# Scan head of a hybrid attention and RWKV-7 trunk: loads reordered, one receptance projection moved ahead of the first slot

## The chip, the cores and the metric

The kernel runs on one NeuronCore of a Trainium2 chip. The metric is the device time of one execution in microseconds (us); lower is better. Five engines work side by side, each on its own list of instructions: PE (TensorE, matrix products; PEld are its weight loads), DVE (VectorE), ACT (ScalarE), POOL (GpSimd) and SP (SyncE), which in this kernel issues every DMA. They wait for one another by semaphores only.

## The reference

Two layers, each of feed-forward, mixer, feed-forward. The mixer of the second layer is RWKV-7 in both directions, and the change lies in it. Cut to what matters here (512 tokens, 1024 channels, 16 heads of 64):

```python
xr, xw, xk, xv, xa, xg = (x + xx * mix[i] for i in range(6))
r = xr @ w_rkv[0]                 # "receptance"
k = xk @ w_rkv[1]
v = xv @ w_rkv[2]
wl = w0 + einsum(tanh(einsum(xw, w1)), w2)
decay = exp(-exp(-softplus(-wl) - 0.5))
a = sigmoid(a0 + einsum(einsum(xa, a1), a2))
...
def step(state, inp):
    r_t, w_t, k_t, v_t, a_t, b_t = inp
    sa = einsum('zbhij,zbhj->zbhi', state, a_t)
    state = state * w_t[..., None, :] + sa[..., None] * b_t[..., None, :] + v_t[..., None] * k_t[..., None, :]
    return state, einsum('zbhij,zbhj->zbhi', state, r_t)
```

Then come a group norm, a bonus term, a gate and a projection by `w_out`.

## The kernel before, in words

The trunk is cut into stages in a row: input, first layer, first feed-forward of the second layer, `rwkv_project` (which ends at about 1432 us of the profile), `Scan` (1432 to about 1870 us), the output projection and the last feed-forward. `rwkv_project` makes k, the decays, the gate and other inputs of the scan and stores them in DRAM: `d_k`, `d_lw` (logarithms of the decays), `d_ah`, `d_iv`, `d_xr`, `d_xv`, `d_g`. Of the receptances it makes only those of head pair 0 (`d_r`); pairs 1 to 7 are made inside the scan.

`Scan` handles the 16 heads as 8 pairs (`hp` 0 to 7), with 8 chunks of 64 tokens in each of two directions (`z`). The work of a pair is split into threads, Python generators whose `yield` ends a step:

- `load(hp)`: k, iv and the raw a2 by DMA, then a2's split into a high and a low part (`a2u`).
- `front(hp, z)` (letters f0, f1): the decay tile `lw` by DMA, a product with `tri` into a PSUM bank of tag a, exponentials on ACT (`e`, `e2`), a three-matmul product of `a2u` with `ah`, then DVE work that builds `ar` and `bk`. It has six steps for z = 0.
- `grams(hp, z)` (g0, g1): products of `bk` and `ar` into banks g, masked by DVE into a unit `xs`, small copies by ACT (`qd`, `qc`), DMAs of halves of the unit (`az<-xs`, then `xs<-ar`).
- `tails` (t0, t1), `values` (v: first a DMA of the weights `wv`, then v from `xv` and `wv`, one of 8 channel chunks a step), `bonus` (b), `invert` (i: one DVE transpose, then 62 small POOL instructions), `inverted` (k), `merge` (j), `turn` (n), `chain` (c), `outputs` (d) and others.
- `receptances` (r): all projections of r for pairs 1, 4, 6, 7, 2, 3, 5. Its DMAs come first (8 chunks of `xr` into `az2` and units 8 and 9, the weights of pair 1 into unit 4, 8 chunks of `xv`, weights of pairs 4, 6 and 7 into units 5 to 7, weights of pairs 2, 3 and 5 into `vt` tiles). Then each projection takes four steps of two channel chunks, in bank y or m, and ends with a copy by ACT (`yt` or `yh`) and a DMA to `d_r`.

A slot n mixes threads of several pairs; the string `SEQ[n]` is the order, one letter a step. Slots -2 and -1 are the lead-in, 0 to 7 the rest. In the scan the orders of PE, ACT and DVE are exactly that of the program (`MANUAL_SCAN`); SP's and POOL's are set by a scheduler at build time, and on the chip each engine runs its list in that order. A DMA that waits on SP therefore holds all DMAs behind it. All DMAs go into one queue; SP uses eight semaphores in turn, so that a DMA waits until the one eight places before it has landed.

Ahead of slot -2, `run` does the whole of `load(0)`, the split of `ah` and the whole of `front(0, 0)`. `unit()` loads the start value `zs` of an inversion.

Of the kernel before, what the change touches and what calls it, by code (L numbers as in the profile page):

```python
# [18 lines left out]
P = 128  # L19
D = 1024  # L20
S = 512
FF = 2816
NF = FF // P
ND = D // P
NT = S // P
# [26 lines left out]
WR_FIRST = (1, 4, 6, 7)  # L52
# [7 lines left out]
SEQ = {  # L60
# [22 lines left out]
def chunks(ap):  # L83
    return ap.rearrange("p (c t) -> p c t", t=CH)
# [900 lines left out]
class Scan:  # L985
# [53 lines left out]
    def receptances(self):  # L1039

        nc = self.nc
        one = lambda ap: ap.rearrange("p a b c d -> p (a b c d)")
        az = self.az[2].rearrange("p a b c -> p (a b c)")
        xr = [h[:, i * S : (i + 1) * S] for h, n in ((az, 4), (one(self.units[-2][0]), 2), (one(self.units[-1][0]), 2)) for i in range(n)]
        for c in range(ND):
            nc.sync.dma_start(xr[c], self.dram["xr"][:, c, :])
        w = {}

        def load(hp, ap):
            w[hp] = ap.rearrange("p (c f) -> p c f", c=ND)  # L1050
            nc.sync.dma_start(w[hp], self.w_r[:, hp * P : (hp + 1) * P].rearrange("(c p) f -> p c f", p=P))

        for hp, i in zip(WR_FIRST, (4, 5, 6, 7)):
            load(hp, one(self.units[i][0]))
            if hp == 1:
                for c in range(ND):
                    nc.sync.dma_start(self.xv[:, c, :], self.dram["xv"][:, c, :])
        rest = [hp for hp in range(1, ND) if hp not in WR_FIRST]
        order = WR_FIRST + tuple(rest)
        while rest:  # L1060
            pair, rest = rest[:2], rest[2:]
            vt = self.tile("vt", [P, NC, 2, 2, CH], 2)
            for i, hp in enumerate(pair):
                load(hp, one(vt)[:, i * D : (i + 1) * D])
        for i, hp in enumerate(order):
            pr = self.k.bank("ym"[i % 2])
            for c in range(ND):
                self.wide(pr, w[hp][:, c, :], xr[c], c == 0, c == ND - 1)
                if c % 2 and c < ND - 1:
                    yield  # L1070
            t = self.tile(("yh", "yt")[hp % 2], [P, S])
            nc.scalar.activation(t, pr, AF.Copy)
            nc.sync.dma_start(self.dram["rkv"][0][:, hp, :], t)
            if hp == order[-1]:
                self.clear(2)
            yield
# [9 lines left out]

    def run(self, late, lead, ln):
        with self.k.tc.manual_schedule(engines=MANUAL_SCAN):
            raw = self.tile("e", [P, S], 2)
            for dst, src in ((raw, self.dram["ah"]), (self.tri, self.consts["tri"])):  # L1090
                self.nc.sync.dma_start(dst, src)
            list(self.load(0))
            self.k.split(self.ah[:, 0, :], self.ah[:, 1, :], raw)
            list(self.front(0, 0))
            for n in ("mask", "onesb"):
                self.nc.sync.dma_start(getattr(self, n), self.consts[n])
            self.zs = []
            for _ in range(2):
                self.unit()
            self.rs, self.out = self.receptances(), self.outs()  # L1100
            self.led, self.stored = [], 0
            for n in range(-2, HEADS // 2):
                if n == HEADS // 2 - 1:
                    self.early.tile([P, 56], F32, name="pad")
                    self.opened.close()
                    late.enter_context(self.k.early())
                    self.lw = self.leads(lead, ln)
                self.slot(n)
            self.ending = self.finish(HEADS // 2 - 1)
            next(self.ending)  # L1110
# [77 lines left out]
    def load(self, hp):  # L1188
# [16 lines left out]
        p.units, p.ar, p.bk = [], [], []  # L1205
        yield

    def front(self, hp, z):

        k, nc, tile_ = self.k, self.nc, self.tile  # L1210
        p = self.st[hp]
        way = slice(None, None, -1) if z else slice(None)
        if z == 0:
            p.r = tile_("r", [P, S], 2)
            nc.sync.dma_start(p.r, self.dram["rkv"][0][:, hp, :])
        lw = tile_("lw", [P, NT, P], 2)
        nc.sync.dma_start(lw, self.dram["lw"][:, z, :, hp * P : (hp + 1) * P])
        pi = k.bank("a")
        for t in range(NT):
            nc.tensor.matmul(pi[:, t * P : (t + 1) * P], lw[:, t, :], self.tri[:, z, :], start=True, stop=True)  # L1220
        yield
        e = tile_("e", [P, S], 2)
        nc.scalar.activation(e, pi, AF.Exp)
        e2 = tile_("e2", [P, S], 2)
        nc.scalar.activation(e2, pi, AF.Exp, scale=-1.0)
        yield
        pa = k.bank("a")
        k.mm3(pa, p.a2u[:, 0, z, :], p.a2u[:, 1, z, :], self.ah[:, 0, :], self.ah[:, 1, :], True, True)
        th = tile_("th", [P, S], 2)
        nc.scalar.activation(th, pa, AF.Tanh, scale=0.5, bias=k.col(C_A0H + z, hp))  # L1230
        ar = tile_("ar", [P, NC, 2, CH], 2)
        bk = tile_("bk", [P, NC, 2, CH], 2)
        at, rt = ar[:, way, 0, :], ar[:, way, 1, :]
        bt, kt = bk[:, way, z, way], bk[:, way, 1 - z, way]
        kc, ec = chunks(p.k), chunks(e)
        if z == 0:
            a1, a0, k1, k0, e1 = at[:, :, 1:], at[:, :, 0:1], kc[:, :, 1:], kc[:, :, 0:1], ec[:, :, : CH - 1]
        else:
            a1, a0, k1, k0, e1 = at[:, :, : 0 : -1], at[:, :, 0:1], kc[:, :, : CH - 1], kc[:, :, CH - 1 :], ec[:, :, 1:]
        nc.vector.scalar_tensor_tensor(a1, k1, k.col(C_NKK, hp), e1, ALU.mult, ALU.mult)  # L1240
        nc.vector.tensor_scalar(a0, k0, k.col(C_NKK, hp), None, ALU.mult)
        end = 0 if z else CH - 1
        ends = ec[:, way, end : end + 1]
        for h in range(2):
            nc.scalar.activation(p.pc[HALF[z], :, h : h + 1], ends[HALF[h]], AF.Copy)
        yield
        nc.vector.tensor_tensor(rt, chunks(p.r), ec, ALU.mult)
        if z == 0:
            nc.vector.scalar_tensor_tensor(p.iv, p.k, k.col(C_KKH, hp), p.iv, ALU.mult, ALU.mult)
        kz = tile_("kz", [P, S], 2)  # L1250
        nc.scalar.activation(kz, th, AF.Identity, scale=k.col(C_KA1, hp), bias=k.col(C_KA2, hp))
        yield
        nc.vector.tensor_tensor(kz, kz, p.k, ALU.mult)
        nc.vector.tensor_tensor(kt, chunks(kz), chunks(e2), ALU.mult)
        yield
        nc.vector.tensor_tensor(e2, p.iv, e2, ALU.mult)
        nc.vector.scalar_tensor_tensor(bt, chunks(th), 1.0, chunks(e2), ALU.add, ALU.mult)
        p.ar.append(ar)
        p.bk.append(bk)
        if z:  # L1260
            yield
            nc.vector.tensor_tensor(kz, p.kz, kz, ALU.add)
        p.kz = kz
        yield
# [436 lines left out]
```

## Time and profile before

| | |
|---|---|
| Time, median of 3 runs | 2250.02 us (2245.41 to 2254.24) |
| Profiled execution | 2249.58 us, of it the span of the instructions 2247.8 us |
| PE busy over the span | 2169.0 us (96%) |
| DVE, ACT, POOL busy | 48%, 43%, 63% |
| DMA | 328.82 MB, 146 GB/s on average |
| Granted TensorE clock, mean | 0.983 of full speed |

The time is a little longer than the span, since an execution also starts and ends outside the instructions. Times inside the profile count from the span's start. A row of the timeline gives start, duration, engine, line of the kernel, operation, tile written <- tiles read, count, and in brackets the idle time of the engine just before and what ended it.

### The profile page before, as it was taken

The page shows a single profiled execution, that of the slowest core. Times are in us where ns is not written, and L with a number is a line of the kernel's source. Part 1 is how long each engine was busy: PE and PEld are TensorE (multiplying, and loading weights), DVE is VectorE, ACT ScalarE, POOL GpSimd, SP SyncE. Part 2 cuts the span into 40 slices and gives each one's busy share as a digit, 9 for nine tenths or more (in the row PEclk, how much of TensorE's full clock was granted, in tenths as well). Part 3 has the DMA queues.
Part 4 walks back from the last instruction along what each step waited for, and adds up shares of the span by engine and source line. Part 5 has one row for each costly group of instructions (what it writes and reads, how often), then busy time and mean ns, then how long its engine had stood idle before and what let it go on. Part 6 is the DMA issues. An engine that isn't in the chain of part 4 may idle for free.

```text
span 2247.8 us, 35130 instructions
## 1 busy us (share of the span) xinstructions
PE 2169.0 (96%) x13784; PEld 1707.8 (76%) x13784; DVE 1068.3 (48%) x1549; ACT 973.8 (43%) x1706; POOL 1425.7 (63%) x1237
## 2 busy tenths in 40 slices
PE   8999999999999999999999988699999998999998
PEld 7888888887888888888888875435667656888886
DVE  2333356276423333743333698425778645232345
ACT  3333345376333333443333435336777633333333
POOL 6878855554487886588887433144776722888854
PEclk9999999999999999999999999799999999999999
DMA  6444463432344445354444534764454642544443
GB/s 199 143 145 145 143 229 97 135 89 91 103 141 150 145 141 174 132 181 137 141 141 132 196 123 155 268 162 117 126 137 111 206 149 94 159 141 141 141 169 122
DMA packets 350497, 328.82 MB, mean 146 GB/s; under 512 B 48458, under 2 KB 277450, under 8 KB 350332
## 3 DMA queue, kind: packets, MB, share of 16 engines
q1 hardware_dynamic: 350332, 326.58, 46.6%
q8 instruction: 108, 1.77, 0.3%
q14 instruction: 57, 0.47, 0.1%
HBM read 262.26 MB, written 47.74 MB: 138 GB/s over the span
## 4 chain that ended last, share of the span: by engine, by line
PE 83%; DVE 7%; DMA 4%; ACT 3%; issue 2%; POOL 1%; SPq 0%; DVEq 0%; ACTq 0%; POOLq 0%
PE bank L800 16%; PE bank L225 16%; PE bank L226 16%; PE bank L227 16%; PE bank L288 4%; PE a L990 3%; PE y L990 1%; PE g L1279 1%; DVE tmp L606 1%; PE m L990 1%; PE bank L1155 1%; DMA late<-in_ffn_w_out_dram 1%; PE g L990 1%; POOL w L221 1%; DMA wv<-in_w_rkv_dram 1%
## 5 line engine op out<-in xcount | busy, mean ns | idle before, releaser
L221 POOL TENSOR_TENSOR w<-raw,w 128x1024 fp32r<-128x1024 f32 (+2 forms) x203 | 507.2, 2500 | 248.3 <-ACT w L220 235.2
L226 PE MATMUL bank<-xT,w 128*128 128x512 f32 x1416 | 551.5, 389 | 1.7 <-DVE xT L221 1.7
L225 PE MATMUL bank<-xT,w 128*128 128x512 f32 x1416 | 552.5, 390 | 0.0
L227 PE MATMUL bank<-xT,w 128*128 128x512 f32 x1416 | 551.2, 389 | 0.0
L220 ACT ACTIVATE w<-raw 128x1024 fp32r<-128x1024 f32 x207 | 218.4, 1058 | 325.5 <-POOL ts L771 126.2
L422 DVE SCALAR_TENSOR_TENSOR ar<-bank,tmp 128x512 f32<-128x512 f32 x88 | 60.9, 692 | 585.1 <-PE bank L227 576.2
L226 PEld LDWEIGHTS bank<-xT,w 128*128 128x128 f32 x1416 | 265.9, 188 | 56.6 <-DVE xT L221 2.5
L227 PEld LDWEIGHTS bank<-xT,w 128*128 128x128 f32 x1416 | 265.8, 188 | 55.1
L225 PEld LDWEIGHTS bank<-xT,w 128*128 128x128 f32 x1416 | 265.9, 188 | 54.3
L1368 POOL TENSOR_TENSOR tm<-qs,zs 128x126 f32<-128x126 f32 (+22 forms) x248 | 104.9, 423 | 133.1 <-DVE qs L1361 83.9
L800 PE MATMUL bank<-wx,an 128*128 128x512 f32 x792 | 187.3, 389 | 0.0
L800 PEld LDWEIGHTS bank<-wx,an 128*128 128x128 f32 x792 | 148.7, 188 | 30.8
L800 PE MATMUL bank<-w,ring 128*128 128x512 f32 x720 | 168.8, 390 | 2.1 <-POOL w L221 2.1
L221 POOL TENSOR_TENSOR wx<-ra,wx 128x512 fp32r<-128x512 f32 x132 | 166.8, 1291 | 3.0 <-ACT wx L220 3.0
L221 DVE TENSOR_TENSOR ring<-ar,ring 128x1024 fp32r<-128x1024 f32 x44 | 122.8, 2792 | 81.3 <-ACT ring L220 81.2
L800 PEld LDWEIGHTS bank<-w,ring 128*128 128x128 f32 x720 | 134.9, 188 | 31.5 <-POOL w L221 3.2
L420 ACT ACTIVATE tmp<-bank 128x512 f32<-128x512 f32 x88 | 52.6, 598 | 231.0 <-PE bank L227 231.0
L221 POOL TENSOR_TENSOR ring<-raw,ring 128x1024 fp32r<-128x1024 f32 x28 | 68.2, 2445 | 96.7 <-ACT ring L220 96.6
L1370 POOL TENSOR_TENSOR zs<-zs,tm 128x126 f32<-128x126 f32 (+22 forms) x248 | 112.6, 454 | 19.4
L220 ACT ACTIVATE wx<-ra 128x512 fp32r<-128x512 f32 x132 | 82.9, 633 | 72.0 <-PE bank L800 67.8
L225 PE MATMUL bank<-xT,ring 128*128 128x256 f32 (+1 forms) x352 | 104.2, 304 | 9.8 <-ACT xT L220 3.7
L221 POOL TENSOR_TENSOR w<-late,w 128x1024 fp32r<-128x1024 f32 x30 | 75.6, 2525 | 58.8 <-ACT w L220 58.8
(284 smaller groups left out, 3779.0 us busy)
## 6 DMA issues: line engine op xcount, KB each, us to landing
raw<-in_ffn_w_in_dram SPq DMA_DIRECT2D x176, 512.0 KB, 3.9
ra<-in_ffn_w_out_dram SPq DMA_DIRECT2D x44, 1024.0 KB, 5.0
late<-d_late SPq DMA_DIRECT2D x34, 512.0 KB, 5.3
late<-in_ffn_w_out_dram SPq DMA_DIRECT2D x28, 512.0 KB, 4.6
raw<-in_w_qkv_dram SPq DMA_DIRECT2D x24, 512.0 KB, 3.9
d_late<-ts SPq DMA_DIRECT2D x44, 256.0 KB, 3.3
d_late<-ra SPq DMA_DIRECT2D x44, 256.0 KB, 2.0
xs<-ar SPq DMA_DIRECT2D x64, 128.0 KB, 2.4
```

Of the source, the lines that this page charges most:

```text
L220: self.hi = self.nc.scalar.activation(h, raw, AF.Copy).ins
L221: self.lo = (eng or self.nc.vector).tensor_tensor(l, raw, h.bitcast(F32), ALU.subtract).ins
L225: nc.tensor.matmul(out, wh, xh, start=start, stop=False)
L226: nc.tensor.matmul(out, wh, xl, start=False, stop=False)
L227: nc.tensor.matmul(out, wl, xh, start=False, stop=stop)
L288: nc.tensor.matmul(acc[t, h], a, u[:, i, h * 512 : (h + 1) * 512], start=first and n == 0, stop=last and n == 2)
L420: nc.scalar.activation(s, pg, AF.Silu)
L422: nc.vector.scalar_tensor_tensor(raw[:, 3:7:3] if j else raw[:, 0:8:7], halves_of(pu), 0.5, halves_of(s), ALU.mult, ALU.mult)
L800: self.nc.tensor.matmul(acc, lhs, u[:, i], start=bool(first) and m == 0, stop=last and m == 2, skip_group_check=more)
L990: self.nc.tensor.matmul(out[hs], w[:, hs], x, start=start, stop=stop)
L1368: nc.gpsimd.tensor_tensor(tv, qs[:, s, 0:s].rearrange("p (a o) -> p a o", o=1).broadcast_to([P, s, n]), zs[:, s : s + 1, c0:].broadcast_to ...
L1370: nc.gpsimd.tensor_tensor(zs[:, 0:s, c0:], zs[:, 0:s, c0:], tv, ALU.add)
```

## The change

1. The head's DMAs are in another order in the program. The decay tile of `front(0, 0)` (`fetch(0, 0)`) and `tri` come first, then k, iv and a2 of pair 0, then `ah`, the receptance tile of pair 0 (`receptance(0)`), the first `xr` chunk, the weights of the first projection, the other `xr` chunks, and among them the decay tile of `front(0, 1)` (`fetch(0, 1)`), `mask` and `onesb`. `xv` and the other projection weights follow at the first `r` step of the head.
2. The four `r` steps of the first projection (pair 1) are done ahead of slot -2, between the steps of `front(0, 0)`: the order is f, then the split of `ah`, then `f f r r f r f r f`.
3. Four `r` steps are taken out of `SEQ[-1]` (9 before, 5 now). Their number over the head and the two slots stays at 28 that do something, so every later projection moves four steps forward.

```diff
-    -1: "f1 v g0 k f1 g0 g0 v r r f1 k r f1 f1 r j f1 g0 l l r g1 r n r g0 g1 f0 g1 j g1 f0 f1 r t0 g1 g1 n g0 v t0 v "
-       "v v f0 v b t1 i f0 t1 v n v f0 f0 r b",
+    -1: "f1 v g0 k f1 g0 g0 v r r f1 k r f1 f1 r j f1 g0 l l r g1 n g0 g1 f0 g1 j g1 f0 f1 t0 g1 g1 n g0 v t0 v "
+       "v v f0 v b t1 i f0 t1 v n v f0 f0 b",
...
@@ receptances
-        for c in range(ND):
-            nc.sync.dma_start(xr[c], self.dram["xr"][:, c, :])
...
+        def chunk(c):
+            nc.sync.dma_start(xr[c], self.dram["xr"][:, c, :])
+
+        chunk(0)
         for hp, i in zip(WR_FIRST, (4, 5, 6, 7)):
             load(hp, one(self.units[i][0]))
-            if hp == 1:
+            if hp == WR_FIRST[0]:
+                for c in range(1, ND):
+                    chunk(c)
+                    if c == 2:
+                        self.fetch(0, 1)
+                        for n in ("mask", "onesb"):
+                            nc.sync.dma_start(getattr(self, n), self.consts[n])
+                yield
                 for c in range(ND):
                     nc.sync.dma_start(self.xv[:, c, :], self.dram["xv"][:, c, :])
@@ run
-            raw = self.tile("e", [P, S], 2)
-            for dst, src in ((raw, self.dram["ah"]), (self.tri, self.consts["tri"])):
-                self.nc.sync.dma_start(dst, src)
-            list(self.load(0))
-            self.k.split(self.ah[:, 0, :], self.ah[:, 1, :], raw)
-            list(self.front(0, 0))
-            for n in ("mask", "onesb"):
-                self.nc.sync.dma_start(getattr(self, n), self.consts[n])
-            self.zs = []
+            self.rs, self.out, self.zs, self.lws, self.rts = self.receptances(), self.outs(), [], {}, {}
+            self.fetch(0, 0)
+            self.nc.sync.dma_start(self.tri, self.consts["tri"])
+            load, start = self.load(0), self.front(0, 0)
+            next(load)
+            raw = self.tile("e", [P, S], 2)
+            self.nc.sync.dma_start(raw, self.dram["ah"])
+            self.receptance(0)
+            next(self.rs)
+            next(load)
+            next(start)
+            self.k.split(self.ah[:, 0, :], self.ah[:, 1, :], raw)
+            for name in "f f r r f r f r f".split():
+                next(start if name == "f" else self.rs)
+            assert next(load, 1) == 1 and next(start, 1) == 1
             for _ in range(2):
                 self.unit()
-            self.rs, self.out = self.receptances(), self.outs()
...
+    def fetch(self, hp, z):
+        lw = self.lws[hp, z] = self.tile("lw", [P, NT, P], 2)
+        self.nc.sync.dma_start(lw, self.dram["lw"][:, z, :, hp * P : (hp + 1) * P])
+
+    def receptance(self, hp):
+        r = self.rts[hp] = self.tile("r", [P, S], 2)
+        self.nc.sync.dma_start(r, self.dram["rkv"][0][:, hp, :])
```

**SP at the head.** What SP issues from the raw `ah` (tile `e`) on, before. The tiles `xs_10779` and, later, `xs_10799`, `xs_10801`, `xs_10790` are units 4 to 7 as homes of projection weights; `az_10807`, `xs_10803` and `xs_10794` are the homes of the `xr` chunks:

```order
L1091 DMA e<-d_ah 128x512
L1354 DMA zs<-in_eye_dram 128x512 x2
L1311 DMA wv<-in_w_rkv_dram 128x8x128
L1217 DMA lw<-d_lw 128x4x128
L1193 DMA k<-d_k 128x512
L1195 DMA iv<-d_iv 64x512 x2
L1197 DMA a2r<-in_a_dram 128x2x128
L1046 DMA az_10807<-d_xr 128x512 x4
L1046 DMA xs_10803<-d_xr 128x512 x2
L1046 DMA xs_10794<-d_xr 128x512 x2
L1051 DMA xs_10779<-in_w_rkv_dram 128x8x128
L1057 DMA xv<-d_xv 128x512 x8
```

And now, from the last `xr` chunks to the k tile of pair 1 (the `xr` chunks, the weights of pair 1, `lw`, `mask` and `onesb` stand ahead of this piece, right behind `ah`):

```order
L1052 DMA xs_10794<-d_xr 128x512 x2
L1066 DMA xv<-d_xv 128x512 x8
L1049 DMA xs_10799<-in_w_rkv_dram 128x8x128
L1049 DMA xs_10801<-in_w_rkv_dram 128x8x128
L1049 DMA xs_10790<-in_w_rkv_dram 128x8x128
L1049 DMA vt<-in_w_rkv_dram 128x8x128 x3
L1378 DMA zs<-in_eye_dram 128x512 x2
L1335 DMA wv<-in_w_rkv_dram 128x8x128
L1207 DMA k<-d_k 128x512
```

`wv`, the weights of the first `values`, stood third behind `ah`; it now stands behind all `xr`, all `xv` and all seven projection weights.

**PE at the head.** Before, from the first product of `front(0, 0)` to the first product of `values(0)`:

```order
L1220 MATMUL a<-tri,lw 128x128 x4
L225 MATMUL a<-ah,a2u 128x512
L226 MATMUL a<-ah,a2u 128x512
L227 MATMUL a<-ah,a2u 128x512
L1279 MATMUL g<-ar,bk 128x128 x8
L1220 MATMUL a<-tri,lw 128x128 x4
L225 MATMUL a<-ah,a2u 128x512
L226 MATMUL a<-ah,a2u 128x512
L227 MATMUL a<-ah,a2u 128x512
L990 MATMUL y<-az_10807,xs_10779 64x512 x8
L1279 MATMUL g<-ar,bk 128x128 x8
L990 MATMUL a<-xv,wv 64x512 x2
```

Now, from the last product of `front(0, 0)` to the same product of `values(0)`:

```order
L227 MATMUL a<-ah,a2u 128x512
L990 MATMUL y<-az_10807,xs_10779 64x512 x8
L990 MATMUL y<-xs_10803,xs_10779 64x512 x4
L990 MATMUL y<-xs_10794,xs_10779 64x512 x4
L1303 MATMUL g<-ar,bk 128x128 x8
L1244 MATMUL a<-tri,lw 128x128 x4
L225 MATMUL a<-ah,a2u 128x512
L226 MATMUL a<-ah,a2u 128x512
L227 MATMUL a<-ah,a2u 128x512
L990 MATMUL m<-az_10807,xs_10799 64x512 x8
L1303 MATMUL g<-ar,bk 128x128 x8
L990 MATMUL a<-xv,wv 64x512 x2
```

The whole projection of pair 1 stands ahead of the first gram, and the second projection (weights `xs_10799`) is where the first one began.

**PE in slot -1.** Before, from the first matmuls of `merge(0)` to the tails of pair 1 (L990 rows with `vt` are receptance steps):

```order
L1401 MATMUL p<-qs,qc 32x32 x32
L1279 MATMUL g<-ar,bk 128x128 x8
L990 MATMUL m<-xs_10794,vt 64x512 x4
L1279 MATMUL g<-ar,bk 128x128 x8
L990 MATMUL y<-az_10807,vt 64x512 x8
L1220 MATMUL a<-tri,lw 128x128 x4
L1408 MATMUL p<-qd,qc 32x32 x32
L1279 MATMUL g<-ar,bk 128x128 x8
L990 MATMUL y<-xs_10803,vt 64x512 x4
L1302 MATMUL g<-ident,bk 128x128 x4
```

Now:

```order
L1425 MATMUL p<-qs,qc 32x32 x32
L1303 MATMUL g<-ar,bk 128x128 x8
L990 MATMUL y<-xs_10794,vt 64x512 x4
L1303 MATMUL g<-ar,bk 128x128 x8
L1244 MATMUL a<-tri,lw 128x128 x4
L1432 MATMUL p<-qd,qc 32x32 x32
L1303 MATMUL g<-ar,bk 128x128 x8
L1326 MATMUL g<-ident,bk 128x128 x4
```

Three receptance steps are gone from here; the fourth, `y<-xs_10794,vt`, stood at the slot's end, ahead of the bonus product. The orders of DVE and POOL are as before; ACT's has only its copies of the projections (`yt`, `yh`) at other places. SP in slot -1 no longer reads a receptance tile back (`r<-d_r`) between iv and the first `az<-xs`, since that tile's read now stands earlier.

More of the change, by code (lines that the diff above doesn't have):

```diff
@@ L1213, in front @@
         if z == 0:
[L1214 to L1217, printed above, removed]
+            if hp:
+                self.receptance(hp)
+            p.r = self.rts.pop(hp)
+        if (hp, z) not in self.lws:
+            self.fetch(hp, z)
+        lw = self.lws.pop((hp, z))
         pi = k.bank("a")
```

## The prediction

> **What bounds the kernel now.** I read the shares by engine first: PE is busy 96% of the span, so PE's own idle time and its slow clock are what an edit of the scan's head can win or lose. Then I cut the head out by stage. Columns: stretch and its length, busy time (count) of PE, PEld, DVE, ACT, POOL, granted clock, DMA share, GB/s.
>
> ```profile
> core 0: us, PE busy (x) PEld busy (x) DVE busy (x) ACT busy (x) POOL busy (x), PEclk, DMA share, GB/s
> 1432.00:1465.00 33.00, 16.04 (x72) 9.31 (x70) 11.57 (x19) 9.18 (x21) 0.00 (x0) 0.59 0.98 306
> 1465.00:1545.00 80.00, 80.00 (x569) 34.26 (x567) 25.37 (x40) 35.65 (x87) 25.62 (x64) 1.00 0.53 143
> 1440.00:1475.00 35.00, 25.79 (x137) 13.65 (x138) 15.76 (x26) 12.83 (x34) 0.00 (x0) 0.72 1.05 305
> ```
>
> In the 33 us of the head PE works 16 and at 0.59 of its clock, while the DMA engines are full. In the 80 us behind it PE is busy without a gap at full clock, so whatever delays the start of that stretch delays all of it. PE's waits in the head (us in total, times, longest), and its timeline:
>
> ```profile
> PE a L1220 <- DMA lw<-d_lw: 8.2, 1, 8.2
> PE g L1279 <- DVE bk L1257: 4.8, 1, 4.8
> PE y L990 <- DMA xs<-in_w_rkv_dram: 3.9, 1, 3.9
> ```
>
> ```profile
> 1440.42 2.05 PE L1220 MATMUL a<-tri,lw 128*128 128x128 f32 x8 [8.16 <-DMA lw<-d_lw]
> ...
> 1443.56 0.63 PE L227 MATMUL a<-ah,a2u 128*128 128x512 f32 x1
> 1449.03 2.08 PE L1279 MATMUL g<-ar,bk 64*128 64x128 f32 x16 [4.85 <-DVE bk L1257]
> ...
> 1453.45 0.40 PE L227 MATMUL a<-ah,a2u 128*128 128x512 f32 x1
> 1457.79 6.38 PE L990 MATMUL y<-az,xs 128*64 128x512 f32 x16 [3.94 <-DMA xs<-in_w_rkv_dram]
> 1464.10 1.16 PE L1279 MATMUL g<-ar,bk 64*128 64x128 f32 x16
> 1465.19 1.08 PE L990 MATMUL a<-xv,wv 128*64 128x512 f32 x4
> ```
>
> The three waits are 17 us. Two end with a DMA in a full queue. The first product of `values` (1465.19) does not wait today: its weights `wv` were issued early.
>
> **The change part by part.**
>
> *The decay tile first, the projection in the gap.* The lw wait of 8.2 us shrinks, but what follows needs `ah`, which is issued at about the same place, so `front(0, 0)` does not end earlier. The four receptance steps then fill the wait for DVE's bk and part of the wait for weights. They are no gain by themselves: they hold up the first gram until the last `xr` chunk is there. What counts is when PE comes to the next point that DMA decides.
>
> *The load of `wv`.* It is now behind all `xr`, `xv`, all seven projection weights and the two `zs`. The queue serves in order: a 64 KB transfer issued behind two big weights took 6.3 us.
>
> ```profile
> 1464.89 1.68 SPq L1051 DMA_DIRECT2D vt<-in_w_rkv_dram  x1
> 1466.67 1.63 SPq L1291 DMA_DIRECT2D az<-xs  x1
> ```
>
> ```profile
> vt<-in_w_rkv_dram SPq DMA_DIRECT2D x1, 512.0 KB, 7.6
> az<-xs SPq DMA_DIRECT2D x1, 64.0 KB, 6.3
> ...
> k<-d_k SPq DMA_DIRECT2D x3, 256.0 KB, 5.0
> iv<-d_iv SPq DMA_DIRECT2D x6, 128.0 KB, 5.0
> a2r<-in_a_dram SPq DMA_DIRECT2D x3, 128.0 KB, 4.1
> ```
>
> From the head's first load to `wv` the new queue holds what the old one held up to its second `vt` weight, less k, two iv and a2r of pair 1 (256 + 256 + 128 = 640 KB), plus the third `vt` weight (512 KB). That is 128 KB less, 0.4 us at 305 GB/s. The old second `vt` weight landed at 1464.89 + 7.6 = 1472.5, so `wv` lands at 1472.1. PE is there long before: between the second projection's weights and `wv` stand 2560 KB of weights, 512 KB of `zs` and `wv` itself, 3584 KB or 12.0 us at 305 GB/s, and PE has between them two receptance steps (3.65 us for such an x16 row at full clock, below) and a gram (1.16). It stands about 7 us at the first product with `wv`, and behind that product, in program order, stand all other grams of slot -2, the inversion on POOL and the rest. That product was at 1465.19: **+6.9 us**. The bounds: 300 to 320 GB/s and the missing k and iv move the landing by about 2.5 us either way, 4.4 to 9.4.
>
> How this stands to PE's work: at 1465.19 today PE has done two receptance steps, at the new point six. Slot -2 has 19 steps before and after, so its length is the same 80 us stretch of PE work, and the four steps come back only in slot -1.
>
> *The clock.* After a wait PE restarts slow. Today's example is in slot -1:
>
> ```profile
> 1553.04 0.79 PE L225 MATMUL a<-ah,a2u 128*128 128x512 f32 x1 [2.66 <-DVE bon L1330]
> ...
> 1673.01 1.08 PE L990 MATMUL a<-xv,wv 128*64 128x512 f32 x4 [2.35 <-DMA wv<-in_w_rkv_dram]
> ```
>
> ```profile
> 1553.00:1559.00 6.00, 5.96 (x33) 3.65 (x33) 2.56 (x7) 1.93 (x4) 5.06 (x13) 0.51 0.28 89
> 1670.00:1680.00 10.00, 7.65 (x115) 5.44 (x115) 6.66 (x14) 6.38 (x18) 8.71 (x17) 1.00 0.45 136
> ```
>
> A wait of 2.66 us is followed by 6 us at 0.51, which costs 6 x 0.49 = 2.9 us; one of 2.35 us is followed by none. A wait of 7 us is beyond both, and at 1465.19 today the clock is already full: **+2.9 us** (0 if it recovered at once, 2.9 by the row). [...]
>
> *Four steps less in slot -1.* At full clock they are 1.8 us each, 7.2 us in all, and PE is busy there:
>
> ```profile
> 1522.95 1.94 PE L990 MATMUL m<-xs,vt 128*64 128x512 f32 x8
> ...
> 1525.91 3.65 PE L990 MATMUL y<-az,vt 128*64 128x512 f32 x16
> ...
> 1532.81 1.94 PE L990 MATMUL y<-xs,vt 128*64 128x512 f32 x8
> ```
>
> But the slot's end is not PE's. The last wait is the 2.66 us above, for DVE's bon, and DVE had itself waited 10.7 us for a DMA:
>
> ```profile
> 1545.53 0.74 DVE L1240 SCALAR_TENSOR_TENSOR ar<-k,cols,e 128x504 f32<-128x504 f32 x1 [10.74 <-DMA xs<-ar]
> ```
>
> That DMA is the last of a chain on SP, `az<-xs`, its landing, `xs<-ar`, three times over:
>
> ```profile
> 1527.58 1.14 SPq L1195 DMA_DIRECT2D iv<-d_iv  x2
> 1529.53 0.33 SPq L1215 DMA_DIRECT2D r<-d_r  x1
> 1529.94 1.38 SPq L1291 DMA_DIRECT2D az<-xs  x2
> ...
> SPq L1073 <- ACT az L1412: 1.4, 1, 1.4
> ...
> SPq L1292 <- DMA az<-xs: 1.8, 1, 1.8
> ```
>
> Fewer PE steps do not shorten the landings. What shortens is the place of `r<-d_r`, which no longer stands between iv (done 1528.72) and `az<-xs` (1529.94), 1.2 us, and the 1.4 us for ACT's az copy, since the products ahead of it move up by two steps. **-2.6 us**; bounds 0 (the landings decide) and 7.2 (PE decides). The steps taken out covered that wait, so PE will stand idle there longer than 2.66 us; its restart is already slow today.
>
> *The rest.*
>
> ```profile
> 1471.85 0.60 ACT L1072 ACTIVATE yt<-y 128x512 f32<-128x512 f32 x1
> ```
>
> I cost it at nothing: the copies `yt` and `yh` on ACT (0.6 us each; ACT is busy 35.65 of 80 us), the earlier `mask` and `onesb` (needed only with the first gram), and the later k, iv, a2 of pair 1, which land 640 KB or 2.2 us behind `wv`, ahead of their first use some 20 us on.
>
> *Sum* on the profiled execution (2249.58 us, of it 2247.8 the span): 6.9 + 2.9 - 2.6 = +7.2, so 2256.8 us. The median of the runs shown is 0.4 us above that execution, so I round to **2257 us**, slower by 0.3%. About 0.5% (11.2 us) is what a measurement of this kernel can tell from no change, and this is within it.
>
> **The rivals.**
>
> *A, faster: `wv` is no gate.* If `wv` lands before PE has done the two steps of the second projection and the gram, PE goes on at about 1465, with no restart, and only the gain of slot -1 is left: 2.6 to 7.2 us, 2242 to 2247. It decides from a landing at 1465, 7 us ahead of my estimate. For it: `wv` alone took 8.0 us today and the head's gaps are real. Against: the queue is full until 1475 and its order does not depend on PE.
>
> *B, slower: slot -1 becomes a latency chain.* With the fillers gone PE waits for DVE's kz and again for bon, each long enough for a slow restart, and the SP chain gains only half a microsecond: 6.9 + 2.9 - 0.5 + 2.9 = +12.2, 2262. It decides once the first of the two waits is over about 2.5 us. For it: DVE's 10.7 us wait, which PE's steps cover today. Against: the restart after the one wait may overlap the other.
>
> *C, the waits cancel.* The stall is at its lower bound (4.4), and slot -1 gives all 7.2: 4.4 + 2.9 - 7.2 = +0.1, 2250. For it: PE is busy without a gap up to 1545. Against: the bon wait.
>
> **How the numbers follow.** Forecast (+3 to +10) 0.48; A 0.17; B 0.22; C 0.09; something faster that I don't see 0.04. A and C lie within 0.5%. Faster by over 0.5% is the last 0.04 and a tail of A, 0.06 together; slower is B and the upper tail of the forecast, 0.27; the same is 0.67. The range reaches from the slow end of A to B with a landing 2 us later: 2246 to 2264.
>
> **What would show it.** Right: PE's first product with `wv` waits about 7 us, ended by that DMA, at about 1472; the clock is near 0.5 for the 6 us behind; slot -2 keeps its length; the wait for bon in slot -1 grows. Wrong: no wait on `wv` (A), or two long waits ahead of bon (B), or a wait for bon that goes away (PE decides there, C). The forecast falls if `wv` lands before 1467, or if the second projection's weights, not `wv`, hold PE longest.

## The result, and the profile after

The changed kernel takes 2266.81 us (median of 4 runs, 2264.73 to 2268.70) against 2252.01 us (2245.41 to 2254.24, 4 runs) before: a ratio of 1.0066, 95% interval 1.0046 to 1.0086. It is slower by 0.5 to 0.9%, above the range that was forecast (2246 to 2264). Its profiled execution took 2268.70 us, 19.1 us more than that of before; a second one, from a later repeat (below), 2265.10 us, 15.5 more.

PE's timeline in the head, after:

```profile
1437.32 1.25 PE L1244 MATMUL a<-tri,lw 128*128 128x128 f32 x8 [2.78 <-DMA tri<-in_tri_dram]
1446.29 0.80 PE L225 MATMUL a<-ah,a2u 128*128 128x512 f32 x1 [7.72 <-ACT ah L220]
...
1448.16 5.46 PE L990 MATMUL y<-az,xs 128*64 128x512 f32 x16
1453.45 3.60 PE L990 MATMUL y<-xs,xs 128*64 128x512 f32 x16
...
1463.75 1.16 PE L1303 MATMUL g<-ar,bk 64*128 64x128 f32 x16
1472.91 1.98 PE L990 MATMUL a<-xv,wv 128*64 128x512 f32 x4 [8.00 <-DMA wv<-in_w_rkv_dram]
1474.65 2.44 PE L990 MATMUL m<-xs,xs 128*64 128x512 f32 x8
1477.02 1.16 PE L1303 MATMUL g<-ar,bk 64*128 64x128 f32 x16
```

The head looks as forecast: the projection fills old gaps, and PE then stands 8.0 us for `wv`, to 1472.91 (forecast: about 7, to 1472.1). At 1477.02 a gram takes 1.16 us again, as at 1463.75; the granted clock is 1.00 at both (1475.70 to 1480.00, 1463.00 to 1468.90). Next, PE's waits from slot -1 to the merge of pair 1 in slot 0, the DVE row that all of slot -1 waits for, DVE's row ahead of the merge, and POOL's first row of the inversion between them:

```profile
1543.79 0.96 PE L1371 MATMUL p<-ident,v 128*128 128x128 f32 x4 [3.96 <-ACT az L1436]
1559.73 0.50 PE L225 MATMUL a<-ah,a2u 128*128 128x512 f32 x1 [0.91 <-DVE bon L1354]
1588.58 1.92 PE L1425 MATMUL p<-qs,qc 32*32 32x32 f32 x64 [1.98 <-DVE qs L1413]
```

```profile
1552.22 0.74 DVE L1264 SCALAR_TENSOR_TENSOR ar<-k,cols,e 128x504 f32<-128x504 f32 x1 [11.91 <-DMA xs<-ar]
1586.74 1.04 DVE L1404 STREAM_TRANSPOSE qd<-zs 128x512 f32<-128x512 f32 x1 [3.32 <-POOL zs L1394]
```

```profile
1555.05 0.54 POOL L1392 TENSOR_TENSOR tm<-qs,zs 128x31 f32<-128x31 f32 x1 [26.28 <-issue]
```

The wait for bon, 2.66 us before, has shrunk to 0.91. New are a wait of 4.0 us for the merge's copy `az` and one of 2.0 us in slot 0, where DVE has stood 3.3 us for the end of POOL's inversion (1555.05 to 1586.74, 31.7 us). Before, the same merge (`p<-qs,qc`) did not wait:

```profile
1582.53 1.20 PE L1401 MATMUL p<-qs,qc 32*32 32x32 f32 x64
```

The largest surprise is some 200 us further on, in slot 6, where the early output projection begins. SP's loads of its weights, and PE's first product with them, after:

```profile
1794.12 0.54 SPq L1516 DMA_DIRECT2D xs<-in_rw_out_dram  x1
1794.75 0.40 SPq L1514 DMA_DIRECT2D bk<-in_rw_out_dram  x1
1795.20 0.42 SPq L1516 DMA_DIRECT2D xs<-in_rw_out_dram  x1
1795.86 0.33 SPq L1505 DMA_DIRECT2D ar<-in_rw_out_dram  x1
1796.28 0.39 SPq L1505 DMA_DIRECT2D wv<-in_rw_out_dram  x1
```

```profile
1804.46 1.97 PE L990 MATMUL a<-wv,xv 128*64 128x512 f32 x4 [5.71 <-DMA wv<-in_rw_out_dram]
```

And the same of before:

```profile
1783.65 0.54 SPq L1490 DMA_DIRECT2D bk<-in_rw_out_dram  x1
1784.27 0.41 SPq L1481 DMA_DIRECT2D wv<-in_rw_out_dram  x1
1784.74 0.43 SPq L1492 DMA_DIRECT2D xs<-in_rw_out_dram  x1
1785.38 0.33 SPq L1481 DMA_DIRECT2D ar<-in_rw_out_dram  x1
1785.76 0.44 SPq L1492 DMA_DIRECT2D xs<-in_rw_out_dram  x1
```

```profile
1788.89 1.98 PE L990 MATMUL a<-wv,xv 128*64 128x512 f32 x4
```

The first output product reads the tile `wv` (which takes over the buffer of the `values` weights). Before, its load was second of five; now it is last, behind four of 512 KB. No line of the edit touches this: the scheduler that sets SP's order at build time chose otherwise, and why it did so stays open. From slot 0 on these five are the only DMAs of the scan whose order on SP differs between the two profiles. The wait-free row of before had no slack either: the load issued at 1784.27 took 4.6 us to land, 1788.87, and the product started at 1788.89. (Its 1.98 us for four matmuls, against 1.08 elsewhere, show that the clock was slow there before, too: 0.50 granted from 1788.80 to 1790.90.)

Stretches at these waits in after, with the columns of the prediction's table by stage (the granted clock is third from the end; the second row is the whole slow stretch around the wait for `wv`):

```profile
1472.00:1478.00 6.00, 5.09 (x28) 2.25 (x28) 0.00 (x0) 0.00 (x0) 0.00 (x0) 0.69 0.99 279
1468.90:1475.70 6.80, 2.79 (x8) 1.05 (x10) 0.00 (x0) 0.00 (x0) 0.00 (x0) 0.50 1.07 293
1588.00:1594.00 6.00, 5.42 (x97) 4.38 (x99) 5.05 (x9) 2.40 (x6) 3.59 (x9) 0.53 0.26 44
1804.00:1812.00 8.00, 7.54 (x48) 3.32 (x50) 0.00 (x0) 1.71 (x4) 6.59 (x19) 0.61 0.13 42
```

To see where the time went I took the start of the same PE instruction in each profile, less its start in the profile of before (us; first column, before's own times). `after_again` and the next three are runs told below:

| PE instruction | before | after | after_again | head_wv | out_wv_first | before_wv_last |
|---|---|---|---|---|---|---|
| last product of `rwkv_project` | 1431.86 | +2.3 | -0.2 | +0.8 | +1.2 | +2.6 |
| first product with `wv` | 1465.19 | +7.7 | +5.4 | -2.1 | +7.1 | 0.0 |
| `a<-kz,onesb`, slot -2 | 1496.6 | +9.1 | +6.8 | -2.1 | +8.9 | 0.0 |
| `p<-ident,v`, start of slot 0 | 1560.2 | +4.0 | +1.6 | -7.1 | +6.8 | -3.9 |
| `p<-ident,v`, behind the merge of pair 1 | 1597.5 | +8.4 | +5.7 | -2.7 | +7.1 | -1.0 |
| `p<-ident,v`, slot 4 | 1753.7 | +9.8 | +6.0 | -1.7 | +5.9 | -1.1 |
| `g<-wv,xv`, second output product | 1796.4 | +17.1 | +12.6 | +4.2 | +8.1 | +5.0 |
| `a<-wv,xv`, slot 7 | 1839.0 | +18.8 | +14.0 | +7.1 | +9.4 | +8.1 |
| `bank<-ident,x`, end of the scan | 1882.18 | +18.9 | +14.1 | +7.3 | +9.5 | +8.1 |

The scan begins up to 3 us apart between executions, with the same code ahead of it. Counted from that beginning, the first product with `wv` stands at 38.7 to 39.2 us in the five profiles whose head is the changed one. In the three with before's head it stands at 33.3 us (before), 30.7 (before_wv_last) and 30.5 (before_four_less, told below). So the profile of before has the latest head of the three, the head's comparison is good to some 3 us, and the columns above, which all lean on that one profile, give the head's loss at its lower end (counted from the beginning it is 5.4 to 8.7 us).

Slot -1 differs between executions too. Up to slot 6 before_wv_last has the same program as before, and PE's start in slot -2 is the same, yet at the start of slot 0 it is 3.9 us earlier. Its wait for bon is shorter (1.19 us, before 2.66), the first product behind it takes 0.50 us (before 0.79, at a granted clock of 0.50), and its merge then waits:

```profile
1551.46 0.50 PE L225 MATMUL a<-ah,a2u 128*128 128x512 f32 x1 [1.19 <-DVE bon L1330]
1580.47 1.20 PE L1401 MATMUL p<-qs,qc 32*32 32x32 f32 x64 [1.71 <-DVE qs L1389]
```

### The profile page after: what moved, and what is told of

The parts are those of the page before. It is cut to its first block, busy times and chain, and to the rows that moved or that the text cites. A ratio compares the mean times of both kernels' runs of the same rounds, so it can differ in the third digit from the quotient of the medians.

```text
span 2266.9 us, 35131 instructions
## 1 busy us (share of the span) xinstructions
PE 2173.9 (96%) x13784; PEld 1708.8 (75%) x13784; DVE 1075.5 (47%) x1549; ACT 973.6 (43%) x1706; POOL 1419.8 (63%) x1237
## 5 line engine op out<-in xcount | busy, mean ns | idle before, releaser
L221 POOL TENSOR_TENSOR w<-raw,w 128x1024 fp32r<-128x1024 f32 (+2 forms) x203 | 500.3, 2466 | 253.3 <-ACT w L220 245.3
L221 DVE TENSOR_TENSOR ring<-ar,ring 128x1024 fp32r<-128x1024 f32 x44 | 133.4, 3031 | 76.3 <-ACT ring L220 76.2
```

The costliest lines, as they stand in the source:

```text
L221: self.lo = (eng or self.nc.vector).tensor_tensor(l, raw, h.bitcast(F32), ALU.subtract).ins
```

## The experiments

All were timed in five rounds against the kernel before on the same chip; its median was 2250.2 to 2252.0 us. The chips differ from run to run, so two kernels are compared here by their ratios to before; the changed kernel's is that of after_again.

**after_again.** The changed kernel, unedited.

> The changed kernel itself, on the chip of the following three. Theory 1: 2264 to 2268 us, a wait of 7 to 8 us at the first product with wv and one of 5 to 6 us at the first output product; slots -1 and 0 together change PE's lag by -3 to 0 us, in whichever of the two PE stands. Theory 2 (one of these waits was an accident of the first profile): it is missing here.

2266.07 us, ratio 1.0069 (1.0057 to 1.0081). Both long waits are there again, 7.9 us for the values' `wv` and 5.8 for the output's. Slots -1 and 0 together gave 1.1 us (table: +6.8 to +5.7). Theory 1 stands.

**head_wv.** Only the place of `wv`'s load:

```diff
@@ receptances, in the loop over WR_FIRST
+            if hp == WR_FIRST[1]:
+                self.value_weights(0)
@@ values
-        wv = tile_("wv", [P, ND, P])
-        nc.sync.dma_start(wv, ...)
+        if hp:
+            self.value_weights(hp)
+        wv = self.wvs.pop(hp)
```

> The changed kernel with one load moved: the weights wv of the first values are issued right behind the weights of the second projection, ahead of those of pairs 6, 7, 2, 3 and 5. Theory 1 (wv's place in the queue is the head's loss): the 8.0 us wait of PE at the first product with wv shrinks below 1 us, that product starts 6 to 8 us earlier against the end of rwkv_project, and the time falls by 5 to 9 us from 2266.8, to 2258 to 2262. Theory 2 (the queue's bytes are the loss): the 512 KB only push back xv or other loads that PE needs next, the stall comes elsewhere in the head, and the time stays within 2 us of 2266.8.

2256.96 us, ratio 1.0029 (1.0019 to 1.0039): 0.40% or 9.0 us less than the changed kernel by the two ratios (1.0069 in after_again). PE's timeline:

```profile
1458.42 3.65 PE L990 MATMUL m<-az,xs 128*64 128x512 f32 x16 [1.68 <-DMA xs<-in_w_rkv_dram]
1462.01 1.16 PE L1310 MATMUL g<-ar,bk 64*128 64x128 f32 x16
1463.10 1.08 PE L990 MATMUL a<-xv,wv 128*64 128x512 f32 x4
```

The 8 us wait is gone, and no other of that size has come in the head: it was the place in the queue, not the bytes. PE is there 2.1 us earlier than in the profile of before, which is within the 3 us by which heads differ, but it has done four more receptance steps by then. Still this kernel is slower than before.

**out_wv_first** and **before_wv_last.** The place of `wv` among the five loads, mended in the changed kernel (SP issues bk, wv, ar, xs, xs) and spoiled in the kernel before (bk, xs, xs, ar, wv). The edits add only edges on the order in which SP issues:

```diff
@@ outs, changed kernel (out_wv_first)
-            nc.sync.dma_start(w[i], rows(self.w_out, i))
+            with self.k.tc.issue_after(first.ins) if i == 2 else nullcontext():
+                ins = nc.sync.dma_start(w[i], rows(self.w_out, i))
+            first = first or ins
...
+                    with self.k.tc.issue_after(first.ins):
                         for c in range(EARLY, ND - 1):
@@ outs, kernel before (before_wv_last); loads collects the DMAs
+                    for j in (2, 4, 5):
+                        self.k.tc.add_manual_dep(loads[0].ins, loads[j].ins.name, ...)
```

> The changed kernel, with the loads of the output projection's weights in about the order of before: bk, wv, ar, xs, xs in place of xs, bk, xs, ar, wv. Theory 1 (the order that the scheduler chose costs a wait far from the edit): the 5.7 us wait of PE at the first output product and the slow clock behind it go away, and the time falls by 6 to 8 us from 2266.8, to 2259 to 2261. Theory 2 (five loads of 512 KB are late in any order): PE waits as long for ar or xs instead, and the time stays within 2 us of 2266.8.

> The kernel before, with only the loads of the output projection's weights in the order of the changed kernel's: wv last. Theory 1: PE waits 4 to 6 us at the first output product, its clock restarts slow, and the time rises by 5 to 8 us from 2252, to 2257 to 2260. Theory 2 (the wait in the changed kernel came from its later scan, not from the order): no wait over 1 us there, and the time stays within 2 us of before.

out_wv_first: 2259.91 us, ratio 1.0047 (1.0030 to 1.0065), 0.22% or 5.0 us less than the changed kernel by the ratios. before_wv_last: 2257.03 us, ratio 1.0039 (1.0024 to 1.0054), 8.8 us more than before by the ratio (the two medians are 6.9 apart). PE's first output product in the one and in the other:

```profile
1796.16 1.98 PE L990 MATMUL a<-wv,xv 128*64 128x512 f32 x4 [1.41 <-DMA wv<-in_rw_out_dram]
```

```profile
1793.31 1.97 PE L990 MATMUL a<-wv,xv 128*64 128x512 f32 x4 [5.42 <-DMA wv<-in_rw_out_dram]
```

This order alone costs the kernel before about as much as it costs the changed one; nothing else of the change is in before_wv_last. So most of what the prediction had at nothing is the order of these loads. The table's step from slot 4 to the second output product is +7.3 and +6.6 in the changed kernel, +6.1 in before_wv_last, +2.2 in out_wv_first.

**invert_early.** In slot -1 the step `i` (DVE's transpose that POOL's inversion of pair 1 waits for) goes ahead of the front step whose DVE work waits 11.9 us:

```diff
-       "v v f0 v b t1 i f0 t1 v n v f0 f0 b",
+       "v v i f0 v b t1 f0 t1 v n v f0 f0 b",
```

> The changed kernel, with the step that starts the inversion of pair 1 (one DVE transpose, then POOL's 62 instructions) moved in slot -1 ahead of the front step whose DVE work waits 11.9 us for a DMA. Theory 1 (POOL's inversion takes back in slot 0 what slot -1 gained): the 2.0 us wait of PE for qs at 1588 and the slow clock behind it go away, PE leaves slot 0 some 5 us earlier, and the time falls to 2261 to 2263. Theory 2 (the next wait is right behind it, for a DMA or the chain): the time stays within 2 us of 2266.8.

2263.28 us, ratio 1.0063 (1.0046 to 1.0079): no difference from the changed kernel that these runs can tell. The wait at the merge is gone (PE's lag is +6.8 at the start of slot 0 and +6.4 behind the merge), but PE had waited more ahead of it, in slot -1:

```profile
1546.16 1.12 PE L1371 MATMUL p<-ident,v 128*128 128x128 f32 x4 [6.33 <-ACT az L1436]
```

out_wv_first, where the inversion is not touched, shows the same wait there (6.45 us) and none at the merge. So the wait stands in one place or the other, and its sum hardly changes: 6.9 us in after (`az`, bon and the merge), 6.3 in invert_early, 6.5 in out_wv_first.

**three_undone** and **wv_and_out.** The edits of head_wv and out_wv_first together, with invert_early's and without.

> The changed kernel with wv's load behind the second projection's weights, the output weights loaded about as before, and the inversion of pair 1 started early: the three edits of the last runs together. Theory 1 (three separate losses): they add, -8.5, -5.5 and -2 from 2265, 2249 us, within 0.2% of before. Theory 2 (they hide one another): 2254 to 2257 us.

> The changed kernel with wv's load behind the second projection's weights and the output weights loaded about as before, the inversion as in the changed kernel. Theory 1 (the losses add, and starting the inversion early is worth 1 to 3 us): 2251 to 2254. Theory 2 (the inversion's place is worth nothing): within 1 us of three_undone, 2250 to 2251.

2250.64 us, ratio 0.9998 (0.9988 to 1.0007), and 2252.29 us, 1.0003 (0.9991 to 1.0016). The two DMA places are worth 0.66% of the changed kernel's 0.69%: they add, and they were nearly all of the loss. The inversion's place, 0.05% here and 0.06% in invert_early, is within the uncertainty.

**before_four_less.** The term of slot -1 by itself, on the kernel before. This kernel leaves out half of each of the last two projections, so it has less work than before:

```diff
+            n = ND // 2 if hp in order[-2:] else ND
-            for c in range(ND):
+            for c in range(n):
@@ SEQ[-1]: the four r of the change taken out
```

> The kernel before with the same four receptance steps taken out of slot -1 and nothing done in the head: the last two of the seven projections are cut to four of their eight channel chunks, so two steps each are left out. This is the term of slot -1 by itself. Theory 1 (the chain of DMAs sets slot -1, and POOL's inversion sets the merge in slot 0): DVE's work behind the last xs<-ar starts 1 to 3 us earlier, PE leaves slot 0 0 to 3 us earlier, and the time falls by 0 to 3 us, 2248 to 2251. Theory 2 (PE sets slot -1): 7 us less, 2243 to 2245.

2249.54 us, ratio 0.9993 (0.9983 to 1.0003): 1.6 us less, not clear of none, and 3.8 at most. In its profile the head is 3.3 us earlier than before's; PE is 6.6 us earlier at the start of slot 0 and 3.5 behind the merge. So in slot -1 this profile gains 3.3 us, and 0.2 is left of it in slot 0. That is no more than before_wv_last shows with all its steps in place (3.9 gained, 1.0 left), so the profile can't tell what the steps gave; the time says that of their 7.2 us of PE's work about half comes back at most. Of PE's timeline, the place where it goes:

```profile
1532.89 1.12 PE L1348 MATMUL p<-ident,v 128*128 128x128 f32 x4 [5.45 <-ACT az L1413]
...
1577.99 1.20 PE L1402 MATMUL p<-qs,qc 32*32 32x32 f32 x64 [1.98 <-DVE qs L1390]
```

**drop_in_slot_m2**, **drop_m2_invert_early** and **head_less_queue.** The four steps are taken out of slot -2 instead; the second starts the inversion early; the third also loads `wv` ahead of `xv` and the second projection's weights, and a2 ahead of k.

```diff
-    -2: "g0 v f1 f1 f1 f1 f1 f1 g0 l g0 r r g0 g0 v r g1 g1 g1 v r g1 v g1 g1 v t0 r g0 ...
+    -2: "g0 v f1 f1 f1 f1 f1 f1 g0 l g0 g0 g0 v g1 g1 g1 v g1 v g1 g1 v t0 r g0 ...
@@ SEQ[-1]: as before the change; wv and the output weights as in wv_and_out
```

> wv's load and the output weights as in three_undone, the inversion where the changed kernel has it; slot -1 keeps its nine receptance steps as before, and the four steps done in the head are taken out of slot -2 (its first four). Theory 1 (slot -1 is set by its chain of DMAs, so steps there are free; in slot -2 PE is the bound): PE comes to slot -1 some 7 us earlier than with the steps in slot -2, the waits of slot -1 are as before, and the time is 2243 to 2247, faster than before by 0.15 to 0.3%. Theory 2 (slot -2 is set by what the full DMA queue brings, or the chain of slot -1 does not move with it): the 7 us come back as waits, 2250 to 2252.

> The last kernel with the inversion of pair 1 started early in slot -1 as well. Theory 1 (POOL's inversion takes back part of what the slots gain): 1 to 4 us less than drop_in_slot_m2. Theory 2 (with slot -1 filled, PE reaches the merge after the inversion's end): within 1 us of it.

> drop_m2_invert_early with two loads moved in the head: wv ahead of xv and of the second projection's weights, a2 ahead of k and iv. Theory 1 (the first product with wv is set by the bytes ahead of it): 1024 KB or more less stand ahead of wv, that product comes 1 to 3 us earlier and the time is 2246 to 2249. Theory 2 (the gram ahead, DVE's mask and ACT's copies set that stretch): within 1 us of 2249.

2253.64 us, 1.0006 (0.9997 to 1.0016); 2249.28, 0.9991 (0.9979 to 1.0002); 2249.14, 0.9993 (0.9981 to 1.0004). My theory fell here: PE reaches the first product with `wv` 5.4 us earlier than before in drop_in_slot_m2, and 3.4 is left behind the merge. Even that flatters it: its profiled execution, 2246.27 us, is the fastest of its 12. In its timeline, what took over in the head and at the merge:

```profile
1463.34 2.67 PE L1310 MATMUL g<-ar,bk 64*128 64x128 f32 x16 [2.51 <-DVE xs L1315]
...
1578.13 1.20 PE L1433 MATMUL p<-qs,qc 32*32 32x32 f32 x64 [2.01 <-DVE qs L1421]
```

In the third, `wv` lands in time and that gram waits 3.75 us for DVE: no gain over the second. The early inversion is worth 0.15% here, at the edge of what the intervals can tell.

**yt_alternate** and **three_undone_yt.** In the profile of after, as in the others told so far that have five receptance steps in slot -1, the merge's copies `az` on ACT stand behind a projection's copy `yt`, and that one waits. ACT's timeline in slot -1, of out_wv_first:

```profile
1540.68 0.60 ACT L1081 ACTIVATE yt<-y 128x512 f32<-128x512 f32 x1 [8.20 <-DMA d_r<-yt]
...
1544.46 1.51 ACT L1436 ACTIVATE az<-p 32x256 f32<-32x256 f32 x4
```

The last two projections, pairs 3 and 5, both go through the one buffer `yt`, and the store of the first stands on SP behind the eight `az<-qd`. (In after the profile puts the same idle time, 5.73 us, down to a gram of PE. The store is issued at 1535.31 and takes 3.0 us to land, and the copy starts at 1538.44, so there too it is the store that fits.) The edit gives the projections `yt` and `yh` in turn:

```diff
-            t = self.tile(("yh", "yt")[hp % 2], [P, S])
+            t = self.tile(("yt", "yh")[i % 2], [P, S])
```

> The changed kernel with the receptance projections' copies going to yt and yh in turn (before: by the pair's number, so that the last two, pairs 3 and 5, both go to yt). Theory 1 (ACT's copy of the last projection waits for the store of the one before it, and the merge's az copy stands behind it): PE's wait of 4 us for az in slot -1 falls below 1 us, DVE's work behind xs<-ar starts 1 to 3 us earlier, PE leaves slot 0 that much earlier, and the time falls by 1 to 3 us from 2266, to 2263 to 2265. Theory 2 (the chain of DMAs sets slot -1 anyway): the wait for az goes away but the one for bon grows by as much, and the time stays within 1 us of 2266.

> three_undone with the copies to yt and yh in turn. Theory 1: the same 1 to 3 us, 2247 to 2249, at or just below before. Theory 2: within 1 us of three_undone, 2250 to 2251.

yt_alternate: 2266.63 us, 1.0064 (1.0051 to 1.0077), the same as the changed kernel. The wait for `az` is gone; these come in its place:

```profile
1552.89 1.69 PE L990 MATMUL a<-kz,onesb 128*64 128x512 f32 x4 [3.71 <-DVE kz L1349]
1558.71 0.50 PE L225 MATMUL a<-ah,a2u 128*128 128x512 f32 x1 [1.05 <-DVE bon L1354]
...
1587.61 1.92 PE L1425 MATMUL p<-qs,qc 32*32 32x32 f32 x64 [2.02 <-DVE qs L1413]
```

Theory 2 holds there: DVE's work behind the last `xs<-ar` starts at 1551.21, 1.0 us earlier than after, with a scan that began 1.0 earlier. three_undone_yt: 2247.54 us, 0.9984 (0.9974 to 0.9994), 0.14% less than three_undone. That is what theory 1 said, though the two intervals overlap a little. DVE's timeline of it shows what may make the same edit count here:

```profile
1533.43 1.25 DVE L1393 STREAM_TRANSPOSE qs<-qd 128x1024 f32<-128x1024 f32 x1 [4.14 <-ACT qd L1319]
1540.80 0.74 DVE L1271 SCALAR_TENSOR_TENSOR ar<-k,cols,e 128x504 f32<-128x504 f32 x1 [6.13 <-DMA xs<-ar]
```

The transpose that starts POOL's inversion now stands ahead of the DMA wait, and follows ACT's `qd` copies, which stand behind `yt` as well; in three_undone it started at 1539.13. From the first product with `wv` to the start of slot 0, PE gains 5.8 us on before's profile here, 3.1 in three_undone and 1.8 in wv_and_out, and in none of the three does slot 0 take any of it back. The profiles can't weigh these gains further: this one is of the fastest of 11 executions (2240.49 us), and slot -1 alone differs by 3.9 us with the same code. By its interval this kernel is 0.06 to 0.26% faster than before.

## Why the prediction was wrong, by its steps

| term (us) | predicted | after | after_again |
|---|---|---|---|
| scan begins later (no step) | 0 | +2.3 | -0.2 |
| wait for `wv` | +6.9 | +5.4 | +5.6 |
| slow clock behind it | +2.9 | +1.4 | +1.4 |
| slots -1 and 0 | -2.6 | -0.7 | -1.1 |
| slots 0 to 4 | 0 | +1.4 | +0.3 |
| slot 6: output weights, clock behind the wait | 0 | +7.3 | +6.6 |
| slot 7: clock behind a stall of 2.1 us | 0 | +1.7 | +1.4 |
| the remainder | 0 | +0.3 | +1.5 |
| sum, against the profile of before | +7.2 | +19.1 | +15.5 |

*The wait for `wv`.* Right in mechanism and place: 8.0 and 7.9 us, ended by that DMA, and head_wv takes it away. The product was forecast at 1472.1 and came at 1472.9 and 1470.6. The +5.4 and +5.6 are against the profile of before; against the other two heads of before, counted from the scan's beginning, they would be some 8 us, so these profiles don't show the +6.9 as mis-sized.

*The clock.* Half the size. I took 6 us at 0.51 from a wait of 2.66 us, and expected no less of a longer one. The slow stretch was as long as the one at bon, 6.8 us at a granted clock of 0.50, but it began at 1468.9, 4.0 us ahead of the product, so PE worked in only 2.8 us of it. Half of these 2.8 us is the 1.4 of the table; a row with PE at work through all 6 us, like the one I took, does not stand for this place.

*Slot -1.* The step that failed here is "-2.6" as a gain that stays; 0.7 and 1.1 stayed. I followed the chain of DMAs to bon and stopped there. DVE's work at that row did start earlier against PE's lag (lag +9.1 in slot -2, DVE +6.7), by 2.4 us, about the amount forecast. But one of its two parts, 1.4 us for ACT's `az` copy, is no property of the kernel. It is a wait of SP at the store `d_r<-yt` in before, and before_wv_last, with the same program there, doesn't have it (below, first before, then before_wv_last); its DVE row is 1.6 us earlier with no change at all.

```profile
1532.05 1.91 SPq L1073 DMA_DIRECT2D d_r<-yt  x1
1531.95 0.59 SPq L1073 DMA_DIRECT2D d_r<-yt  x1
```

And the same DVE queue holds the transpose that starts POOL's inversion, 31.7 us long, and the merge in slot 0 comes right behind its end. In the seven profiles in which that transpose stands behind the DVE row and PE waits at the merge, the merge starts 36.4 to 36.5 us behind the row. In before it is 37.0, without a wait, so only half a microsecond was free there: what PE gains in slot -1 beyond the row, it waits at the merge. In after that wait was 2.0 us, with a clock of 0.53 over 6 us. The named sign, a longer wait for bon, was wrong: PE waits earlier, for `az`, and the wait for bon shrank. "The copies `yt` and `yh` on ACT" were costed at nothing by their 0.6 us; in their new place ACT stands 5.7 to 8.2 us ahead of one of them, until a store has landed, with the merge's copies behind it. Mended alone (yt_alternate) it is worth nothing, so the zero was right for the time and wrong for the reason.

*"The rest" at nothing.* This is the step that put the result outside the range. Up to the merge in slot 0 the forecast was +7.2 and the two profiles show +6.1 and +5.9 beyond the scan's start. That they are so near is in part luck: the wait and its clock came 3.0 and 2.8 us short of their sum, and slot -1 gave 1.9 and 1.5 less than its term. Behind it I had no term, and 10.7 and 9.8 us came, 7.3 and 6.6 of them at one place: the order of SP's five loads of output weights, over 200 us behind the edit. I read SP's new order in the head and in slot -1 and took the rest as unchanged, though it is a list that the scheduler makes anew. before_wv_last shows the cost with nothing else changed, out_wv_first most of it taken away. Slot 7's row is not the edit's: out_wv_first, head_wv and before_wv_last have 1.3 to 3.1 us there too.

*The rivals.* A falls by the 8.0 us wait. B had the right thought, that slot -1 becomes a chain of waits that gives back half a microsecond (measured 0.7 to 1.1). A second restart did come ahead of bon, but behind the wait for `az` and not for kz, with a clock of 0.72 over the 6 us behind it; the restart at bon went away (1.00 over the 6 us from 1559.7), and another came at the merge (0.53). Its sum, 2262, is near what these terms give without the output weights (2265.1 less 6.6 is 2258.5; 2268.7 less 7.3 is 2261.4), but not by its own steps. C falls: the wait for bon did almost go away, the sign named for it, but slot -1 kept 1 us and not 7.2.

## What to carry to other kernels

Where a scheduler sets an engine's order, read its whole new list against the old one, far behind the edit too, and look at each moved load for how long before its use it landed: a row without a wait may have a slack of 0.02 us. A gain inside a pipelined stage is followed to the next point where a long off-path stretch (here POOL's 31.7 us) meets the path, and counts only if that stretch starts earlier as well. And a term read from a single profile is checked against a second one of the same program: here slot -1 alone differed by 3.9 us.

## What the runs showed of the hardware

In these runs a stall's cost in clock did not grow with its length. PE's rows behind the same instruction in slot 7, before and in after_again:

```profile
1826.49 0.18 PE L1408 MATMUL p<-qd,qc 32*32 32x32 f32 x1 [2.17 <-issue]
1826.60 0.45 PE L1441 MATMUL c<-wr,az 64*64 64x64 f32 x8
```

```profile
1839.04 0.21 PE L1432 MATMUL p<-qd,qc 32*32 32x32 f32 x1 [2.12 <-issue]
1839.18 0.69 PE L1465 MATMUL c<-wr,az 64*64 64x64 f32 x8
```

Stalls of 2.17 and 2.12 us: behind the one the clock is full (0.45 us for eight small products, 1.00 granted from 1826.6 to 1832.6), behind the other it is not (0.69 us, 0.73 granted from 1839 to 1845), and 1.4 us are lost. The wait of 8.0 us cost 1.4 us, that of 1.98 us at the merge some 2.8. The granted clock shows why. The stretch at 0.50 was 6.8 us long both at `wv` in after (the second of the rows by stage, in the section on the result) and at bon in before (below), with 1.00 just ahead of it and behind it, and what counts is how much of it PE works: 2.8 us and 5.9.

```profile
1552.10:1558.90 6.80, 5.86 (x31) 3.60 (x31) 3.46 (x9) 1.93 (x4) 5.76 (x14) 0.50 0.30 96
```

The slow stretch began 4.0 us ahead of the product at `wv` (1468.9 and 1472.91, in after) and 0.9 us ahead of the one at bon (1552.1 and 1553.04, in before). Nor did the length of a stall tell whether a slow clock followed. Behind gaps of 1.55 us (the merge in after_again), 1.98 (the merge in after) and 2.12 the clock was 0.54, 0.53 and 0.73 over 6 us. Behind gaps of 1.68 us (in after, at 1759.98), 2.17 and 2.35 (in before, at 1673.01) it was 1.00 over 6 us. I had taken the restart as a function of the wait; for a sum it is better, as an estimate from these rows, a term of 0 to 2.9 us for each stall like these, of 1.55 to 8.0 us.
